# The mixers' triangular inverse on smaller tiles of the array, its substitution on GpSimd, and the last chain's rank

## The chip, the cores and the metric

The kernel runs on one core of one Trainium2 chip. The core has TensorE (matrix products), VectorE and ScalarE (element-wise work), GpSimd, SyncE (which here only issues DMAs) and 16 DMA engines. The metric is the device time of one execution in microseconds; where several executions are shown it is their median.

## The reference

Two transformer-like blocks run one after the other on one sequence of 256 tokens with 2048 features, all in float32. The first has a gated linear recurrence, an attention with forget gates and a pooling branch, then a feed-forward network. The second normalises, projects once, and runs two mixers on the projection: an RWKV-7 recurrence over 16 heads of 64 and a gated delta rule over 8 heads of 128; then an output product and a feed-forward network. The change touches only the mixers. What they compute is this:

```python
def rwkv7_recurrence(r, w, k, v, a, b):
    def step(S, inp):
        r_t, w_t, k_t, v_t, a_t, b_t = inp
        Sa = jnp.einsum('bhvk,bhk->bhv', S, a_t)
        S = S * w_t[:, :, None, :] + Sa[..., None] * b_t[:, :, None, :] + v_t[..., None] * k_t[:, :, None, :]
        return S, jnp.einsum('bhvk,bhk->bhv', S, r_t)
...
def gated_delta_rule_chunked(q, k, v, g, beta):
    ...
    L = jnp.where(strict, jnp.einsum('bhnid,bhnjd->bhnij', k_beta, k) * gamma, 0.0)
    rhs = jnp.concatenate([v_beta, k_beta * jnp.exp(g)[..., None]], axis=-1)
    sol = lax.linalg.triangular_solve(L + eye, rhs, left_side=True, lower=True, unit_diagonal=True)
...
y_a, v_first = rwkv7_mixer(p_rwkv, ...)
y_b = gdn_mixer(p_gdn, ...)
y = jnp.concatenate([y_a, y_b], axis=-1).astype(x.dtype)
x = x + y @ w_out[l]
```

The kernel computes both recurrences in two chunks of 128 tokens. In each chunk and head the dependence of a token on the earlier ones is a triangular matrix of 128 x 128 with ones on its diagonal, which has to be inverted: 32 of them for RWKV, 16 for the delta rule.

## The kernel before

Nearly all the time is products with streamed weights. A weight tile of 128 x 1024 float32 (512 KB) comes from DRAM as `raw` (L310). ScalarE rounds it to `hi` (L314), VectorE takes the rest as `lo` (`sub`, L206), and TensorE multiplies a 512-column product with `hi` and a 256-column one with `lo` (`product`, `mm`, L233) for each 128 x 128 block. The activations `h` are split in the same way. These products write tiles called `ps`; below they are the main stream. About 0.35 us of TensorE go by for one pair of them.

The mixers (`mixers`) run between about 1600 and 2117 us. Four rounds `g` each have an RWKV group (two heads in each of two fronts, so eight matrices, `ab`) and a gated-delta group (one front, four matrices, `gab`). A front makes its projections with the main stream and then a small graph that ends in the matrices; RWKV's come from the products `pf<-ar,bt` and `pf<-ar,kt`. After a group's front, `diagonals` starts on its 16 x 16 diagonal blocks: eight DMAs bring them to DRAM (`scr`, L1105), one brings them back with one block on each partition (`d`, L1107), 15 steps of a back substitution of a product and an addition each invert all blocks at once (`etmp`, `e`, on VectorE), and two DMAs bring the result through DRAM (`scs`, L1122) to `cmp` (L1124), a column of blocks for each matrix.

While the next group's front runs, `step` works off the group before: `merged_inverse` for four matrices at a time (two calls for an RWKV group, one for a gated-delta group, so three in a round and twelve in all), and behind it the rest of the chain (`rwkv_back`, `gdn_back`), which writes the mixer's output. An inverse call takes the 16-row blocks to 32, 64 and 128 rows. Each of the first two levels masks the matrix, multiplies twice (four products of 128 x 128 each time, on `pb` tiles) and transposes; the last one works with 64 x 64 quarters. A float32 product is two passes on TensorE.

The order of instructions on each engine is set when the program is built, by a scheduler that takes the code's order and a rank: `back_ahead = 205`, `diag_ahead = 129` and the like put what stands in a `high_priority` block so many places ahead. So the products of the chains stand in between products of the main stream, and where one of them has to wait, the main stream behind it on TensorE waits too. SyncE issues the weight loads and the DMAs of `diagonals` in one queue. The last group's chain runs beside `out2_first`, the first part of the output product.

Of the kernel before, what the change touches and what calls it, by code (L numbers as in the profile page):

```python
# [7 lines left out]
F32 = mybir.dt.float32  # L8
# [7 lines left out]
P = 128  # L16
# [135 lines left out]
def constants():  # L152
    i = np.arange(P)
    r, c = i[:, None], i[None, :]
    sel1 = np.zeros((P, 8), np.float32)
    sel2 = np.zeros((P, 8), np.float32)
    for h in range(8):
        sel1[h, h] = 1.0
        sel2[32 + h, h] = 1.0
    c1 = ((i >= 32) & (i < 40)).astype(np.float32)[:, None]  # L160
    c2 = (i < 8).astype(np.float32)[:, None]
    up = (c > r).astype(np.float32)
    upi = (c >= r).astype(np.float32)
    same = lambda b: (r // b == c // b)
    lev = lambda b: (same(2 * b) & ~same(b) & (c > r)).astype(np.float32)
    return [
        ("ident", np.eye(P)), ("ones", np.ones((P, P))),
        ("causal", np.where(c <= r, 0.0, -1e30)), ("causalT", np.where(r <= c, 0.0, -1e30)),
        ("head64", same(64).astype(np.float32)),
        ("nsel1", -sel1), ("sel2", sel2), ("c1", c1), ("c2", c2),  # L170
        ("atmask", np.concatenate([up, upi], 1)),
        ("lev16", lev(16)), ("lev32", lev(32)), ("lev64", lev(64)), ("blk16", same(16).astype(np.float32)),
        ("id16", np.broadcast_to(np.eye(16).reshape(1, 256), (P, 256))),
    ]


def ffn_out(w):
# [5 lines left out]
class Prog:  # L183
# [95 lines left out]
    def setup(self):  # L279
        nc, a = self.nc, self.a  # L280
        self.const = self.pool("const", 1)
        self.rawp, self.hip, self.lop = (self.pool(n, b) for n, b in zip(("raw", "hi", "lo"), self.rings))
        self.evp = self.pool("ev", 3)
        self.bigp = self.pool("big", 1)
        self.psum = self.pool("psum", 8 - sum(self.pbufs), PSUM)
        self.psx = self.pool("psx", 1, PSUM)
        self.dram = self.pool("dram", 1, DRAM)
        self.par = self.const.tile([P, a["par"].shape[1]], F32, name="par")
        self.cst = self.const.tile([P, a["cst"].shape[1]], F32, name="cst")
# [505 lines left out]
class Block2(Block1):  # L795
# [102 lines left out]
    def mixers(self, rh, st):  # L898
# [3 lines left out]
        self.gp = self.pool("mxg", 1, st=st)  # L902
        self.parted = True
        self.narrow = self.nar3
        ps = self.product([(w2[0], KT)], rh)
        self.norm2_end()
        self.omu = kp.tile([P, 27], F32, name="omu")
# [25 lines left out]
            self.step(pend, first=True)  # L933
        self.narrow = self.nar4
        self.out2_first()
        self.step(pend)

    def step(self, pend, first=False):
# [14 lines left out]
                        self.gdn_back(g, fr, xx)  # L953

    back_ahead = 205
    diag_ahead = 129
    front_ahead = 0

    def shifted(self, ps, o, j):

        t = self.w(S + 1, "shf")
        self.G.memset(t[:, 0:1], 0.0)
        self.scaled(ps, t[:, 1:])
        self.act(o, t[:, 1:], AF.Copy, scale=self.omu[:, j:j + 1])
        self.stt(o, t[:, :S], self.p("mu_rkv", j), o, ALU.mult, ALU.add)
# [39 lines left out]
    def rwkv_rest(self, j, slot, t, slots):  # L1005
# [5 lines left out]
        self.G.memset(cw[:, :, 0:1], 0.0)  # L1011
# [86 lines left out]
    def diagonals(self, slots, gdn):  # L1098
# [15 lines left out]
        self.V.tensor_copy(x, self.c("id16")[:8 * n].rearrange("p (i j) -> p i j", i=16))  # L1114
# [12 lines left out]
    def merged_inverse(self, slots, half, gdn):  # L1127

        full, cm, p0 = slots["ab"], slots["cm"], 4 * half
        q4 = lambda z: z.rearrange("p (q t) -> p q t", q=4)  # L1130
        xt = self.gp.tile([P, 4, P], F32, name="xt", tag="xt", bufs=2)
        x = self.gp.tile([P, 4, P], F32, name="xn", tag="xn", bufs=2)
        self.mul(xt.rearrange("p q (b j) -> p q b j", b=8),
                 cm[:, p0:p0 + 4].rearrange("p q (a j) -> p q a j", a=1).to_broadcast([P, 4, 8, 16]),
                 self.c("blk16").rearrange("p (a b j) -> p a b j", a=1, b=8).to_broadcast([P, 4, 8, 16]))
        px = self.psx_tile(True)
        for q in range(4):
            self.tr(px[:, q * P:(q + 1) * P], xt[:, q])
        self.A.copy(x, q4(px))
        beta = lambda q, rows=slice(0, P): self.nbt[rows, q % 2, 2 * gdn + q // 2:2 * gdn + q // 2 + 1]  # L1140
        for lev in ("lev16", "lev32"):
            off = self.tp.tile([P, 4, P], F32, name="off", tag="w4")
            self.mul(off, full[:, p0:p0 + 4], self.bc(lev, 4))
            pm = self.psx_tile(True)
            for q in range(4):
                self.mm(pm[:, q * P:(q + 1) * P], off[:, q], x[:, q])
            m1 = self.tp.tile([P, 4, P], F32, name="m1", tag="w4")
            pt = self.psx_tile(True)
            if gdn is None:
                self.add(m1, q4(pm), self.bc("ident", 4))  # L1150
            else:
                for q in range(4):
                    self.act(m1[:, q], pm[:, q * P:(q + 1) * P], AF.Copy, scale=beta(q))
            for q in range(4):
                self.mm(pt[:, q * P:(q + 1) * P], m1[:, q], xt[:, q])
            if gdn is None:
                self.A.copy(xt, q4(pt))
            else:
                self.add(xt, q4(pt), xt)
            px = self.psx_tile(True)  # L1160
            n = P if lev == "lev16" else 64
            for q in range(4):
                self.T.transpose(px[:n, q * n:(q + 1) * n], xt[:n, q, :n], self.c("ident")[:n, :n])
            self.A.copy(x[:n, :, :n], q4(px[:n, :4 * n]))

        lo, hi = slice(0, 64), slice(64, P)
        pm = self.psx_tile(True)
        for q in range(4):
            self.mm(pm[hi, q * 64:(q + 1) * 64], full[lo, p0 + q, hi], x[lo, q, lo])
        m1 = self.tp.tile([P, 4, P], F32, name="m1", tag="w4")  # L1170
        if gdn is None:
            self.A.copy(m1[hi, :, :64], q4(pm[hi, :S]))
        else:
            for q in range(4):
                self.act(m1[hi, q, :64], pm[hi, q * 64:(q + 1) * 64], AF.Copy, scale=beta(q, hi))
        for q in range(4):
            self.mm(pm[lo, S + q * 64:S + (q + 1) * 64], m1[hi, q, :64], xt[hi, q, hi])
        self.A.copy(xt[lo, :, hi], q4(pm[lo, S:]))
        return xt

# [89 lines left out]
    def gdn_front(self, i, rh, w2, slots):  # L1270
        gp = self.gp

        big = gp.tile([P, 6, S], F32, name="gbig", tag="gbig")
        for b in range(6):
            ps = self.product([(w2[27 + 6 * i + b], KT)], rh)
            if b >= 4:
                self.scaled(ps, big[:, b])
                continue
            t = self.w(S + 3, f"gc{b}")
            self.G.memset(t[:, :3], 0.0)  # L1280
# [155 lines left out]
```

## Time and profile before

| | |
|---|---|
| median of 3 runs | 2921.1 us (2919.22 to 2923.79) |
| the profiled execution's own time | 2924.65 us |
| its span | 2922.9 us |
| its mean granted clock | 0.998 of full speed |
| TensorE, VectorE, ScalarE, GpSimd busy | 99%, 68%, 52%, 1% |
| mean DMA rate | 176 GB/s |

The span is cut into stretches by time: the two that matter for the change are the mixers' from 1606 to 2117 us and, inside it, the first inverse at 1686 us. Rows of an engine in order of time have the start, the duration, the engine, the line of the kernel, the operation, the names written and read, and, in brackets, how long the engine was idle before it and what ended that. Successive products overlap on TensorE, so the time that one takes from the engine is read from start to start and not from its duration.

### The profile page before, as it was taken

The numbers are of one execution on the slowest core, as the hardware profiler recorded it, in microseconds if no ns is written. First come the engines' busy times: TensorE is split into PE (matmuls) and PEld (weight loads), VectorE is DVE, ScalarE is ACT, GpSimd is POOL, SyncE is SP. The second block draws the span as 40 slices with busy tenths as digits, with TensorE's granted clock in tenths as the row PEclk, the third lists the DMA queues.
The fourth block names the chain that finished last, engine by engine and source line by source line (L and its number), as shares of the span: only waits on it lengthen the run. The fifth ranks groups of instructions, "written<-read, shape, count | busy, mean of one in ns | idle before, by whom it ended". The sixth has DMA issues, their size and how long they took to land. (4 is left out here: it accounts for less than half of the span.)

```text
span 2922.9 us, 46401 instructions
## 1 busy us (share of the span) xinstructions
PE 2888.2 (99%) x17676; PEld 2540.8 (87%) x17676; DVE 1990.9 (68%) x3393; ACT 1506.3 (52%) x2448; POOL 21.5 (1%) x88
## 2 busy tenths in 40 slices
PE   8999999999999999999999999999999999999998
PEld 8999988888888888888888878887888888888887
DVE  7855766666766665666667878888776665566665
ACT  6644454444554444444556555666564444444454
POOL 0000000000000000000000000000010000000000
PEclk9999999999999999999999999999999999999999
DMA  6544555555655556555565423233465555655554
GB/s 232 183 160 154 173 188 191 190 188 189 231 190 189 189 177 192 201 191 191 180 206 186 148 87 122 92 130 110 145 207 189 190 186 182 201 191 190 184 177 159
DMA packets 178047, 515.78 MB, mean 176 GB/s; under 512 B 32024, under 2 KB 59040, under 8 KB 177568
## 3 DMA queue, kind: packets, MB, share of 16 engines
q1 hardware_dynamic: 177536, 511.80, 51.9%
q8 instruction: 138, 2.26, 0.3%
q10 hardware_dynamic: 288, 1.02, 0.1%
q14 instruction: 85, 0.70, 0.1%
HBM read 505.66 MB, written 7.09 MB: 175 GB/s over the span
## 5 line engine op out<-in xcount | busy, mean ns | idle before, releaser
L233 PE MATMUL ps<-h,hi 128*128 128x512 f32 (+1 forms) x5904 | 1801.0, 366 | 1.2 <-DVE xp L206 0.9
L206 DVE TENSOR_TENSOR lo<-raw,hi 128x1024 fp32r<-128x1024 f32 (+2 forms) x1028 | 1156.6, 1125 | 759.0 <-ACT hi L314 754.9
L314 ACT CAST hi<-raw 128x1024 fp32r<-128x1024 f32 (+2 forms) x1028 | 997.2, 971 | 1193.3 <-issue 663.8
L233 PE MATMUL ps<-h,lo 128*128 128x256 f32 x5152 | 1410.6, 282 | 0.9 <-DVE lo L206 0.6
L233 PEld LDWEIGHTS ps<-h,hi 128*128 128x128 f32 x5904 | 1041.6, 188 | 164.4 <-issue 6.0
L233 PEld LDWEIGHTS ps<-h,lo 128*128 128x128 f32 x5152 | 969.5, 188 | 29.4 <-issue 2.4
L233 PE MATMUL ps<-mid,hi 128*128 128x512 f32 (+1 forms) x1452 | 486.2, 385 | 0.0
L233 PE MATMUL ps<-mid,lo 128*128 128x256 f32 x1408 | 386.1, 281 | 0.0
L233 PEld LDWEIGHTS ps<-mid,hi 128*128 128x128 f32 x1452 | 265.4, 188 | 50.5
L233 PEld LDWEIGHTS ps<-mid,lo 128*128 128x128 f32 x1408 | 265.1, 188 | 5.3
L206 DVE TENSOR_TENSOR t<-ps,s 128x256 f32<-128x256 f32 x323 | 134.8, 417 | 0.0
L381 ACT COPY s<-ps 128x256 f32<-128x256 f32 x323 | 118.3, 367 | 0.0
L233 PE MATMUL ps<-merged,hi 128*128 128x512 f32 x256 | 88.0, 392 | 0.0
L233 PE MATMUL ps<-merged,lo 128*128 128x256 f32 x256 | 69.0, 280 | 0.0
L233 PEld LDWEIGHTS ps<-merged,hi 128*128 128x128 f32 x256 | 47.0, 188 | 9.6 <-DVE merged L206 0.2
L233 PE MATMUL ps<-y,hi 128*128 128x512 f32 (+1 forms) x160 | 49.3, 359 | 1.7 <-ACT hi L314 1.4
L233 PEld LDWEIGHTS ps<-merged,lo 128*128 128x128 f32 x256 | 48.1, 188 | 1.3
L233 PE MATMUL ps<-yg,hi 128*128 128x512 f32 (+1 forms) x160 | 48.6, 354 | 0.0
L233 PE MATMUL ps<-yb,hi 128*128 128x512 f32 x128 | 46.1, 393 | 0.0
L233 PE MATMUL ps<-yc,hi 128*128 128x512 f32 x128 | 46.1, 393 | 0.0
L233 PE MATMUL ps<-ya,hi 128*128 128x512 f32 x128 | 45.9, 391 | 0.0
L206 DVE TENSOR_TENSOR t<-ps,xres 128x256 f32<-128x256 f32 x78 | 33.1, 424 | 12.9 <-PE ps L233 7.0
(383 smaller groups left out, 2307.8 us busy)
## 6 DMA issues: line engine op xcount, KB each, us to landing
raw<-wg SPq DMA_DIRECT2D x352, 512.0 KB, 4.2
raw<-w SPq DMA_DIRECT2D x292, 512.0 KB, 3.6
raw<-wd SPq DMA_DIRECT2D x128, 512.0 KB, 3.5
raw<-wbr SPq DMA_DIRECT2D x48, 512.0 KB, 3.5
raw<-wo SPq DMA_DIRECT2D x48, 512.0 KB, 4.3
raw<-wd SPq DMA_DIRECT2D x128, 192.0 KB, 3.1
raw<-wo SPq DMA_DIRECT2D x32, 256.0 KB, 3.2
xin<-x SPq DMA_DIRECT2D x4, 512.0 KB, 6.4
```

What stands on the lines that cost most here:

```text
L206: return (e or self.V).tensor_tensor(out=o, in0=x, in1=y, op=op)
L233: return self.T.matmul(o, lhsT=l, rhs=r, start=start, stop=stop, skip_group_check=True)
L314: self.A.copy(hi, raw)
L381: self.A.copy(s[:rows], ps[:rows, S:])
```

## The change

Three things change, and some small ones with them.

1. `merged_inverse` no longer works on 128 x 128 matrices. The blocks of a level stand as [128, 4, 32] or [128, 4, 64], one block below the other. Products of 32 x 32 or 64 x 64 use only the rows and columns of TensorE at that block (`tiles`). The first transpose is VectorE's, in blocks of 32; the others fall away, since each level computes both the blocks and their transposes (`merge`). The masks of 128 columns go, and smaller constants come.
2. In `diagonals` the substitution runs on GpSimd. It also copies the blocks above the diagonal that the two levels multiply into tiles `off` that are zeroed once. Three small memsets go from GpSimd to VectorE (L962, L1011 and L1280 of before).
3. The last chain gets the rank 2000 where the others have 205.

The constants' tile has 320 columns less of content and 320 of padding, so it is as large as before.

```diff
...
-        ("lev16", lev(16)), ("lev32", lev(32)), ("lev64", lev(64)), ("blk16", same(16).astype(np.float32)),
+        ("id64", np.tile(np.eye(64), (2, 1))), ("id32", np.tile(np.eye(32), (4, 1))),
+        ("blk16", diag_blocks(same(16).astype(np.float32), 32)), ("blk32", diag_blocks(same(32).astype(np.float32), 64)),
...
+        self.offs = {}
+        for n in (8, 4):
+            for w in (32, 64):
+                off = self.offs[n, w] = kp.tile([P, n, w], F32, name=f"off{n}_{w}")
+                self.G.memset(off, 0.0)
...
         self.out2_first()
+        self.back_ahead = self.last_ahead
         self.step(pend)
...
     back_ahead = 205
+    last_ahead = 2000
     diag_ahead = 129
...
-        self.G.memset(t[:, 0:1], 0.0)
+        self.V.memset(t[:, 0:1], 0.0)
...
-            self.stt(d, d, -1.0, nb.to_broadcast([8 * n, 16, 16]), ALU.mult, ALU.mult)
+            self.ts(nb, nb, -1.0, e=self.G)
+            self.mul(d, d, nb.to_broadcast([8 * n, 16, 16]), self.G)
...
-            self.mul(o, d[:, :t, t:t + 1].to_broadcast([8 * n, t, w]), x[:, t:t + 1, t:].to_broadcast([8 * n, t, w]))
-            self.add(x[:, :t, t:], x[:, :t, t:], o)
+            self.mul(o, d[:, :t, t:t + 1].to_broadcast([8 * n, t, w]), x[:, t:t + 1, t:].to_broadcast([8 * n, t, w]), self.G)
+            self.add(x[:, :t, t:], x[:, :t, t:], o, self.G)
...
+        for w in (32, 64):
+            off = slots[w] = self.offs[n, w]
+            for r in range(0, P, w):
+                up, right = slice(r, r + w // 2), slice(r + w // 2, r + w)
+                self.G.tensor_copy(off[up, :, w // 2:], full[up, :, right])
...
+        def tiles(out, left, right, w, rows=P):
+            for q in range(4):
+                for r in range(0, rows, w):
+                    r = slice(r, r + w)
+                    self.mm(out[r, q], left[r, q], right[r, q])
+
+        def merge(x, w, rows):
+
+            off = slots[w][:, p0:p0 + 4]
             pm = self.psx_tile(True)
...
+            tiles(q4(pm[:, :4 * w]), off, x[:, 1], w)
+            m = self.tp.tile([P, 4, 64], F32, name="m1", tag="m4", bufs=3)[:, :, :w]
             if gdn is None:
...
+                self.add(m, q4(pm[:, :4 * w]), one(self.c(f"id{w}"), w))
             else:
                 for q in range(4):
...
+                    self.stt(m[:, q], pm[:, q * w:(q + 1) * w], beta(q), self.c(f"id{w}"), ALU.mult, ALU.add)
+            pt = self.psx_tile(True)
+            pt = pt[:, :8 * w].rearrange("p (a q t) -> p a q t", a=2, q=4)
+            tiles(pt[:, 0], m, x[:, 0], w)
+            tiles(pt[:, 1], x[:, 0], m, w, rows)
+            return pt
+
+        xt = self.gp.tile([P, 4, P], F32, name="xt", tag="xt", bufs=2)
+        self.V.memset(xt[hi, :, lo], 0.0)
+        x = self.gp.tile([P, 2, 4, 32], F32, name="xa", tag="xa", bufs=2)
...
+        self.V.transpose(x[:, 1].rearrange("p q t -> p (q t)"), x[:, 0].rearrange("p q t -> p (q t)"))
+        pt = merge(x, 32, P)
+        x = self.gp.tile([P, 2, 4, 64], F32, name="xb", tag="xb", bufs=1)
+        for j in range(2):
+            self.mul(x[:, j].rearrange("p q (b t) -> p q b t", b=2),
+                     pt[:, j].rearrange("p q (b t) -> p q b t", b=1).to_broadcast([P, 4, 2, 32]),
+                     self.c("blk32").rearrange("p (a b t) -> p a b t", a=1, b=2).to_broadcast([P, 4, 2, 32]))
+        pt = merge(x, 64, 64)
+        for r in (lo, hi):
+            self.A.copy(xt[r, :, r], pt[r, 0])
+        y = self.tp.tile([P, 4, 64], F32, name="xc", tag="m4", bufs=3)
+        self.V.tensor_copy(y[lo], pt[lo, 1])
...
```

TensorE, first inverse call of the second round, before: `pb` rows are the inverse's, `ps` rows the main stream's; the rows left out between them are main-stream products.

```order
L236 MATMUL pb<-cst,xt 128x128 x4
...
L233 MATMUL pb<-xn,off 128x128 x4
...
L233 MATMUL pb<-xt,m_18602 128x128 x4
...
L1163 MATMUL pb<-cst,xt 128x128 x4
...
L233 MATMUL pb<-xn,off 128x128 x4
...
L233 MATMUL pb<-xt,m_18623 128x128 x4
...
L1163 MATMUL pb<-cst,xt 64x64 x4
...
L233 MATMUL pb<-xn,ab 64x64 x4
...
L233 MATMUL pb<-xt,m_18642 64x64 x4
```

Nine groups, the two quarter products at the end among them. In this round 174 main-stream products stand between the last `ar,kt` product and the first row of this fence; in the other rounds it is 141, 174 and 168.

The same call on TensorE, after:

```order
L238 MATMUL pb<-xa,off_32_15951 32x32 x16
...
L238 MATMUL pb<-xa,m_18746 32x32 x16
L238 MATMUL pb<-m_18746,xa 32x32 x16
...
L238 MATMUL pb<-xb,off_64_15953 64x64 x8
...
L238 MATMUL pb<-xb,m_18793 64x64 x8
L238 MATMUL pb<-m_18793,xb 64x64 x4
...
L238 MATMUL pb<-xc,ab 64x64 x4
...
L238 MATMUL pb<-xt,m_18817 64x64 x4
```

Three transposes and four groups of 128 x 128 products have gone, and four groups of small products have come. The first row now stands 115 main-stream products behind the last `ar,kt` one (in the four rounds 125, 115, 119 and 109). In the second gated-delta group 67 products stand between the last `kq` product and the first one of the inverse, where 99 stood.

SyncE's queue in the second round, before: `raw<-w` are weight loads, the others the DMAs of `diagonals`.

```order
L1105 DMA scr_18147<-ab 16x8x16 x8
L310 DMA raw<-w 128x1024 x2
L1107 DMA d<-scr_18147 64x256
L310 DMA raw<-w 128x1024 x6
L1122 DMA scs_18191<-e 64x256
L310 DMA raw<-w 128x1024
L1124 DMA cmp<-scs_18191 128x8x16
```

The load of the blocks stands behind two weight loads, and the write of the inverted blocks behind six more.

The same place on SyncE, after:

```order
L1118 DMA scr_18279<-ab 16x8x16 x8
L316 DMA raw<-w 128x1024
L1120 DMA d<-scr_18279 64x256
L316 DMA raw<-w 128x1024 x3
L1136 DMA scs_18323<-e 64x256
L316 DMA raw<-w 128x1024
L1138 DMA cmp<-scs_18323 128x8x16
```

One weight load fewer stands ahead of the load of the blocks, and three instead of six ahead of the write. Whatever the write waits for, the weight loads behind it wait for too.

GpSimd in the mixers, after (before, there are only memsets here): a gated-delta group's copies and the start of its substitution.

```order
L1128 COPY e<-cst 32x256
L1145 COPY off_32_15955<-gab 16x4x16 x4
L1145 COPY off_64_15957<-gab 32x4x32 x2
L211 TENSOR_TENSOR d<-d,nbd 32x256
L211 TENSOR_TENSOR etmp<-d,e 32x15
L211 TENSOR_TENSOR e<-e,etmp 32x15
L211 TENSOR_TENSOR etmp<-d,e 32x14x2
L211 TENSOR_TENSOR e<-e,etmp 32x14x2
```

The copies stand before the first operation that needs the blocks back. GpSimd's rows of a group stand together; among those of a gated-delta group there is one small operation on the next group's `nbd`.

## Rows read from the trace of the kernel before

**Rows 1.** The page: busy time by engine, and one costly group.

```profile
PE 2888.2 (99%) x17676; PEld 2540.8 (87%) x17676; DVE 1990.9 (68%) x3393; ACT 1506.3 (52%) x2448; POOL 21.5 (1%) x88
...
L206 DVE TENSOR_TENSOR t<-ps,s 128x256 f32<-128x256 f32 x323 | 134.8, 417 | 0.0
```

**Rows 2.** Stretches: length, busy PE, PEld, DVE, ACT, POOL, clock, DMA share, GB/s.

```profile
1606.00:2117.00 511.00, 502.56 (x3161) 414.80 (x3160) 405.20 (x1015) 301.17 (x605) 4.85 (x44) 1.00 0.37 119
1683.00:1686.20 3.20, 0.43 (x3) 0.10 (x1) 0.68 (x2) 1.36 (x3) 0.00 (x0) 0.96 0.63 233
1686.20:1690.00 3.80, 3.73 (x18) 3.44 (x19) 2.75 (x6) 1.18 (x3) 0.10 (x1) 0.59 0.07 25
```

**Rows 3.** TensorE in order of time at the first inverse.

```profile
1686.27 1.11 PE L236 MATMUL pb<-cst,xt 128*128 128x128 f32 x4 [2.84 <-DVE xt L206]
```

**Rows 4.** TensorE in order of time, 1717 to 1724 us.

```profile
1717.22 0.39 PE L233 MATMUL ps<-h,hi 128*128 128x512 f32 x1
1717.45 1.07 PE L233 MATMUL pb<-xn,off 128*128 128x128 f32 x8
...
1718.48 0.40 PE L233 MATMUL ps<-h,hi 128*128 128x512 f32 x1
...
1721.12 0.39 PE L233 MATMUL ps<-h,hi 128*128 128x512 f32 x1
1721.44 0.41 PE L1163 MATMUL pb<-cst,xt 64*64 64x64 f32 x4
...
1722.01 0.40 PE L233 MATMUL ps<-h,hi 128*128 128x512 f32 x1
...
1722.36 0.39 PE L233 MATMUL ps<-h,hi 128*128 128x512 f32 x1
1722.68 0.68 PE L233 MATMUL pb<-xn,ab 64*64 64x64 f32 x8
...
1723.51 0.39 PE L233 MATMUL ps<-h,hi 128*128 128x512 f32 x1
```

**Rows 5.** TensorE in order of time at 2011 us.

```profile
2011.34 0.48 PE L233 MATMUL pf<-ar,bt 64*128 64x256 f32 x1
2011.34 0.48 PE L233 MATMUL pf<-ar,kt 64*128 64x256 f32 x1
2011.66 0.38 PE L233 MATMUL pf<-ar,bt 64*128 64x256 f32 x1
```

**Rows 6.** Instructions on tile etmp: ns shortest/median/longest, first and last start, forms.

```profile
L206 DVE TENSOR_TENSOR etmp<-d,e x120: 152/198/220, 1666.3 to 2089.0; 64x15 f32<-64x15 f32 x8, 64x28 f32<-64x28 f32 x8, 64x39 f32<-64x39 f32 x8, 64x48 f32<-64x48 f32 x8
```

**Rows 7.** TensorE in order of time, second round.

```profile
1771.20 0.80 PE L233 MATMUL pf<-ar,kt 64*128 64x256 f32 x3
...
1804.57 0.66 PE L236 MATMUL pb<-cst,xt 128*128 128x128 f32 x4
```

**Rows 8.** VectorE in order of time, second round.

```profile
1784.14 0.18 DVE L206 TENSOR_TENSOR etmp<-d,e 64x15 f32<-64x15 f32 x1 [0.62 <-DMA d<-scr]
```

**Rows 9.** SyncE's queue in order of time, second round.

```profile
1773.18 3.66 SPq L1105 DMA_DIRECT2D scr<-ab  x8
1776.94 2.85 SPq L310 DMA_DIRECT2D raw<-w  x2
1780.06 0.47 SPq L1107 DMA_DIRECT2D d<-scr  x1
1782.11 15.01 SPq L310 DMA_DIRECT2D raw<-w  x6
1798.40 0.46 SPq L1122 DMA_DIRECT2D scs<-e  x1
```

**Rows 10.** GpSimd's groups: count | busy us, mean ns | idle us before, releasers.

```profile
L206 POOL TENSOR_TENSOR acc<-acc,q 128x256 f32<-128x256 f32 x15 | 13.8, 920 | 154.7 <-ACT q L230 154.7
L962 POOL MEMSET shf<- 128x1 f32 x27 | 2.8, 110 | 1550.9 <-PE pf L233 1096.2 <-PE ps L233 424.3 <-DVE rs_w L206 14.2
```

**Rows 11.** TensorE's groups by shape: the first transposes.

```profile
L236 PE MATMUL pb<-cst,xt 128*128 128x128 f32 x48 | 8.4, 292 | 3.5 <-DVE xt L206 3.5
```

More of the change, by code (lines that the diff above doesn't have):

```diff
@@ L164, in constants @@
     same = lambda b: (r // b == c // b)
-    lev = lambda b: (same(2 * b) & ~same(b) & (c > r)).astype(np.float32)
     return [
@@ L171, in constants, with diag_blocks @@
         ("atmask", np.concatenate([up, upi], 1)),
-        ("lev16", lev(16)), ("lev32", lev(32)), ("lev64", lev(64)), ("blk16", same(16).astype(np.float32)),
+        ("id64", np.tile(np.eye(64), (2, 1))), ("id32", np.tile(np.eye(32), (4, 1))),
+        ("blk16", diag_blocks(same(16).astype(np.float32), 32)), ("blk32", diag_blocks(same(32).astype(np.float32), 64)),
         ("id16", np.broadcast_to(np.eye(16).reshape(1, 256), (P, 256))),
     ]
+def diag_blocks(m, n):
+    return np.concatenate([m[i:i + n, i:i + n] for i in range(0, P, n)], 0)
 def ffn_out(w):
@@ L288, in setup @@
         self.par = self.const.tile([P, a["par"].shape[1]], F32, name="par")
-        self.cst = self.const.tile([P, a["cst"].shape[1]], F32, name="cst")
+        self.cst = self.const.tile([P, a["cst"].shape[1] + 320], F32, name="cst")[:, :a["cst"].shape[1]]
         nc.scalar.dma_start(out=self.par, in_=a["par"])
@@ L1010, in rwkv_rest @@
         cw, e1, e2 = (ch(self.w(2 * (P + 1), n)) for n in ("cw", "e1", "e2"))
-        self.G.memset(cw[:, :, 0:1], 0.0)
+        self.V.memset(cw[:, :, 0:1], 0.0)
         for c in range(2):
@@ L1125, in diagonals @@
         slots["cm"] = cm
+        for w in (32, 64):
[3 more added lines that the diff above has]
+                self.G.tensor_copy(off[up, :, w // 2:], full[up, :, right])
     def merged_inverse(self, slots, half, gdn):
         full, cm, p0 = slots["ab"], slots["cm"], 4 * half
+        lo, hi = slice(0, 64), slice(64, P)
         q4 = lambda z: z.rearrange("p (q t) -> p q t", q=4)
-        xt = self.gp.tile([P, 4, P], F32, name="xt", tag="xt", bufs=2)
@@ L1132, in merged_inverse @@
[L1132 to L1139, printed above, removed]
-        beta = lambda q, rows=slice(0, P): self.nbt[rows, q % 2, 2 * gdn + q // 2:2 * gdn + q // 2 + 1]
@@ L1141, in merged_inverse @@
-        for lev in ("lev16", "lev32"):
-            off = self.tp.tile([P, 4, P], F32, name="off", tag="w4")
-            self.mul(off, full[:, p0:p0 + 4], self.bc(lev, 4))
+        one = lambda z, w: z.rearrange("p (a t) -> p a t", a=1).to_broadcast([P, 4, w])
+        beta = lambda q, rows=slice(0, P): self.nbt[rows, q % 2, 2 * gdn + q // 2:2 * gdn + q // 2 + 1]
+        def tiles(out, left, right, w, rows=P):
[3 more added lines that the diff above has]
+                    self.mm(out[r, q], left[r, q], right[r, q])
@@ L1144, in merged_inverse @@
+        def merge(x, w, rows):
+            off = slots[w][:, p0:p0 + 4]
             pm = self.psx_tile(True)
[L1145 to L1148, printed above, removed]
+            tiles(q4(pm[:, :4 * w]), off, x[:, 1], w)
+            m = self.tp.tile([P, 4, 64], F32, name="m1", tag="m4", bufs=3)[:, :, :w]
             if gdn is None:
-                self.add(m1, q4(pm), self.bc("ident", 4))
+                self.add(m, q4(pm[:, :4 * w]), one(self.c(f"id{w}"), w))
@@ L1151, in merged_inverse @@
             else:
                 for q in range(4):
[L1153 to L1163, printed above, removed]
@@ new lines, in merged_inverse @@
+        self.V.memset(xt[hi, :, lo], 0.0)
+        x = self.gp.tile([P, 2, 4, 32], F32, name="xa", tag="xa", bufs=2)
+        self.mul(x[:, 0].rearrange("p q (b j) -> p q b j", b=2),
+                 cm[:, p0:p0 + 4].rearrange("p q (a j) -> p q a j", a=1).to_broadcast([P, 4, 2, 16]),
+                 self.c("blk16").rearrange("p (a b j) -> p a b j", a=1, b=2).to_broadcast([P, 4, 2, 16]))
+        self.V.transpose(x[:, 1].rearrange("p q t -> p (q t)"), x[:, 0].rearrange("p q t -> p (q t)"))
+        pt = merge(x, 32, P)
@@ L1167, in merged_inverse @@
+        self.V.tensor_copy(y[lo], pt[lo, 1])
         pm = self.psx_tile(True)
         for q in range(4):
-            self.mm(pm[hi, q * 64:(q + 1) * 64], full[lo, p0 + q, hi], x[lo, q, lo])
-        m1 = self.tp.tile([P, 4, P], F32, name="m1", tag="w4")
+            self.mm(pm[hi, q * 64:(q + 1) * 64], full[lo, p0 + q, hi], y[lo, q])
+        m1 = self.tp.tile([P, 4, 64], F32, name="m1", tag="m4", bufs=3)
         if gdn is None:
-            self.A.copy(m1[hi, :, :64], q4(pm[hi, :S]))
+            self.A.copy(m1[hi], q4(pm[hi, :S]))
@@ L1173, in merged_inverse @@
         else:
             for q in range(4):
[L1175 removed]
+                self.act(m1[hi, q], pm[hi, q * 64:(q + 1) * 64], AF.Copy, scale=beta(q, hi))
         for q in range(4):
[L1177 removed]
+            self.mm(pm[lo, S + q * 64:S + (q + 1) * 64], m1[hi, q], xt[hi, q, hi])
         self.A.copy(xt[lo, :, hi], q4(pm[lo, S:]))
@@ L1279, in gdn_front @@
             t = self.w(S + 3, f"gc{b}")
-            self.G.memset(t[:, :3], 0.0)
+            self.V.memset(t[:, :3], 0.0)
             self.scaled(ps, t[:, 3:])
```

4 lines of the change are left out of this document (1 added, 3 removed).

## The prediction

> **What bounds the kernel now.** I read the page first, then busy times by stretch, then the order of time on TensorE, VectorE and SyncE inside the mixers, since every edit lies there. TensorE is busy for 99% of the span, VectorE for 68% [rows 1]. The stretch from 1606 to 2117 us holds the eight mixer groups and the first part of the output product. In it TensorE is busy 502.56 of 511 us, so 8.4 us is all the idle time that relief elsewhere can give back; VectorE is at 405 us there, ScalarE at 301, GpSimd at 4.85 [rows 2]. So the change pays by what it takes off TensorE's own row of work, and costs by every wait that it puts into it. One wait is there already: at the first inverse TensorE stands 2.84 us until the diagonal blocks are back [rows 3]. In the 3.8 us behind it the granted clock is 0.59, so mostly the lower of its two levels (1.2 and 2.4 GHz), which costs 0.41 x 3.8 = 1.6 us more [rows 2].
>
> **The change part by part.**
>
> *The products of the inverse.* It is called twelve times (three calls in each of four rounds). A call is nine groups on TensorE now, and seven are replaced: three of transposes and four of four 128x128 products (eight passes, two to each fp32 product). The last two, 64x64, stay. I price a group from the start of the 512-wide product ahead of it to the start of the one behind it, less 0.35 us for the two products that fall in between anyway; this takes in the drain and the weights that could not be loaded ahead. Four products: 1718.48 - 1717.22 - 0.35 = 0.91 us. The 64-row transposes: 1722.01 - 1721.12 - 0.35 = 0.54. A 64x64 group of eight passes: 1723.51 - 1722.36 - 0.35 = 0.80 [rows 4]. I take the 128-row transposes at 0.54 too. Removed per call: 4 x 0.91 + 3 x 0.54 = 5.26 us.
>
> Added per call are four groups: 16 products 32x32, then 32 of them, then eight 64x64, then twelve. A 128-column pass takes 0.91 / 8 = 0.114, so a 64-column one half of that, 0.058 rounded up, and 0.80 - 8 x 0.058 = 0.34 us is the fixed price of a small-tile group. Passes on different row tiles run side by side: the `ar,bt` and `ar,kt` products stand on two halves of the rows and start in the same hundredth of a microsecond, 0.48 long each, the next pair 0.32 later [rows 5]. No row has a 32-row tile. By halving again, a pass takes 0.032; the bounds are 0.008 (four side by side) and 0.058 (nothing gained from the shorter row), and I take 0.012, between two and four side by side. That gives 0.34 + 32 x 0.012 = 0.72 and 0.34 + 64 x 0.012 = 1.11, and for the 64-row groups (two side by side, but the last eight passes on one tile) 0.34 + 16 x 0.029 = 0.80 and 0.34 + 16 x 0.029 + 8 x 0.058 = 1.27. Sum 3.90 us, saved 1.36 per call, 16.3 in twelve. The new order cuts groups into pieces at twelve more places (0.34 each, 4.1); the old one cut a few cheaper ones, so I charge 3.5. **TensorE: -12.8 us.**
>
> *The substitution on GpSimd.* In each of eight groups 30 dependent small operations leave VectorE, 0.198 us each [rows 6]. VectorE's 47 us are worth nothing by themselves, since TensorE's work hides them. What counts is when the blocks come back. In the second round the chain of now is: the last product that feeds it, from 1771.20 to 1772.00 [rows 7], eight DMAs out, one back, the first operation at 1784.14 [rows 8], the DMA behind the last at 1798.40 [rows 9], one more DMA, the transposes at 1804.57 [rows 7]. Without the substitution that is 12.1 + 6.2 = 18.3 us. The new order has one weight load less ahead of the DMA back, on which SyncE stood until 1780.06 [rows 9], so I take 17.0. GpSimd's two-input operation on 256 elements takes 0.920 us, its memset of one column 0.110 [rows 10]. The new ones have 15 to 64 elements, 45 on average: by a straight line 0.25 us. I take 0.24, or 7.2 us for thirty; the bounds are 3.3 (all like the memset) and 27.6 (all like the large one).
>
> So the blocks are needed 17.0 + 7.2 = 24.2 us after the last product that feeds them. In the new order TensorE arrives sooner: between the last `ar,kt` and the first product of the inverse stand 125, 115, 119 and 109 products of the main stream in the four rounds, where 141, 174, 174 and 168 stood. At 0.35 us a pair, and 1.5 us of other work, that is 23.3, 21.6, 22.3 and 20.5 us: waits of 0.9, 2.6, 1.9 and 3.7, in sum 9.1, less 3.0 for the first one's of now: +6.1. The gated-delta groups have more work in between; only the second is tight (67 products where 99 stood), and I put its wait at 2.3, from 0 to 4. Behind TensorE's waiting product stands the main stream, behind VectorE's the split of the next weights, behind SyncE's waiting DMA the weight loads; a ring of four loads is held ahead, each worth 2.8 us of products, so a few microseconds there are covered. **Waits: +8.4 us.** One wait of about 3 us is there before and after, so the clock's 1.6 us stay.
>
> A rule that speaks against this edit: the Trainium skill (GPSIMD Engine Reference, 4.1 Engine selection) puts element-wise work on VectorE, as GpSimd is about twice as slow with two inputs. The trace agrees: 0.920 us against VectorE's 0.417 at 128x256 [rows 1, 10]. By that rule thirty operations would take 11.8 us and the whole change some 25 us more than now.
>
> *The rest.* 51 memsets of 0.1 us go from GpSimd to VectorE, hidden as above. VectorE and ScalarE lose masks, adds and copies over 128x512 for pieces a quarter or half as large; six copies per group go to GpSimd and stand before the substitution, while its data travel. All this is bounded by TensorE's idle time outside the counted wait, 8.4 - 3.0 = 5.4 us; I credit half. **Relief: -2.5 us**, from 0 to -5.4. The last chain, ranked first, ends earlier, but the second part of the output product starts only when the first has ended, so that earns nothing: the chain's cover is that first part. If its blocks are late it costs a wait like the others, at most the 3.7 above.
>
> **Sum:** -12.8 + 8.4 - 2.5 = -6.9 us. The profiled execution took 2924.65 us (span 2922.9, 1.75 around it), which gives 2917.8; the median of the three runs shown lies 3.5 us lower, at 2921.1, and gives 2914.
>
> **Rivals.**
>
> *GpSimd too slow (slower).* If it stands to VectorE as at 256 elements, 0.920 / 0.417 = 2.2 times 0.198, an operation takes 0.44 us and the substitution 13.1. The rounds wait 17.0 + 13.1 less TensorE's way: 6.8, 8.5, 7.8 and 9.6, in sum 32.7, less 3.0; the second gated-delta group waits 8.2, the last about 4. That is +41.9, and four more waits long enough for the clock to fall as it does now, +6.4. With -12.8 and -2.5 it gives +33: 2954. It decides from where the five waits eat the 6.9 us, 1.4 each: 8.6 us for thirty, 0.29 an operation. For it: the steps depend on each other, and a busy VectorE reads the same memory. Against: VectorE itself needed 14.3 us for 5.9 us of operations, since they stood between others, and GpSimd has nothing else to do.
>
> *Small tiles don't run side by side (slower).* At 0.032 a 32-row pass and 0.058 a 64-row one the groups take 1.36, 2.39, 1.27 and 1.73: 6.75 per call, 1.49 more than what goes. Twelve calls +17.9, cuts +3.5, waits +8.4, relief -2.5: +27, 2948. At 0.058 for all it is 2978. For it: the rows show two tiles side by side and never four, and these two write different tiles of the accumulator. Against: nothing in the new groups depends on another tile.
>
> The Trainium skill (TensorEngine Tiling (Array Packing), Gotcha 1: PSUM Pressure) says that different row tiles cannot access one PSUM bank at the same time. The new groups write one bank from four row tiles, on different partitions; no row here shows that case. By that rule this rival would come true.
>
> *All fits (faster still).* Four side by side (-17.5 with the cuts), no wait left at the blocks (-3.0 and the clock's -1.6), the idle time given back (-5.4): -27, 2894. For it: the order of now is well timed, since in all twelve calls TensorE idled 3.5 us at the first transposes, 2.84 of it in the first [rows 3, 11], and the new one may be so again.
>
> **How the numbers follow.** The forecast has 0.42, with a range of its own from 2904 to 2923; GpSimd too slow 0.27; no overlap 0.13; all fits 0.18. A change under 0.2% (5.8 us) can't be told from none. Of the forecast's share about 0.25 lies beyond that, 0.17 within; of the slow GpSimd's 0.04 lies within. So faster 0.43, same 0.21, slower 0.36. The range reaches from the good case to near the bad ones: 2893 to 2950.
>
> **What would show it.** Right: 32x32 groups of 0.7 to 1.1 us, GpSimd's operations at about 0.24 us from start to start, waits of 1 to 4 us at the inverse's first product, VectorE's busy time some 50 us lower. Wrong: steps of 0.3 us or more with waits over 5 us and a lower clock behind them, or 32x32 groups over 1.4 us.

## The result: slower by 1.9%, and where the time went

The changed kernel takes 2975.8 us (median of 5 runs, 2972.6 to 2979.4) against 2921.1 before: 1.0187 times as long, interval 1.0176 to 1.0198. The forecast was 2914, its range 2893 to 2950. What came true is the first rival, "GpSimd too slow", which had a chance of 0.27 and a time of 2954, and it came at a higher price than it was given.

First the page and the waits of the kernel after (engine, tile and line, what it waited for; us in total, times, longest), beside [rows 1, 11]:

```profile
PE 2886.3 (97%) x18780; PEld 2528.7 (85%) x18780; DVE 1954.2 (66%) x3252; ACT 1482.3 (50%) x2389; POOL 143.2 (5%) x345
```

```profile
DVE xa L211 <- DMA cmp<-scs: 58.3, 8, 10.5
PE pb L238 <- DVE xa L1186: 51.6, 6, 10.8
PE pb L238 <- DVE z L211: 5.5, 2, 3.3
```

TensorE idles 51.6 us at the first product of an inverse where it idled 3.5 before, in six places, and 5.5 at two later products of the chain (`pb<-z,xt`), where no wait stood before. It is busy about as long as before, although it has less to do. The busy times by stretch show why (columns as in [rows 2]; the mixers are longer now, and the second and third rows are 4 us around the end of two of the waits, 0.6 to 0.7 us of the wait and the work behind it):

```profile
1606.00:2166.00 560.00, 500.84 (x4257) 401.78 (x4255) 364.24 (x862) 274.54 (x545) 122.49 (x302) 0.94 0.35 106
...
1809.30:1813.30 4.00, 3.27 (x73) 2.60 (x77) 2.11 (x6) 0.00 (x0) 0.00 (x0) 0.50 0.48 174
...
2079.30:2083.30 4.00, 3.40 (x98) 2.95 (x102) 2.08 (x8) 1.87 (x2) 0.00 (x0) 0.50 0.42 99
```

At each of the six waits such a stretch of 4 us has a granted clock of 0.50 to 0.57, so it is near its lower level. The same place on TensorE in the second round, which [rows 7] shows for before:

```profile
1799.94 0.39 PE L238 MATMUL ps<-h,hi 128*128 128x512 f32 x1
1810.03 0.66 PE L238 MATMUL pb<-xa,off 32*32 32x32 f32 x32 [9.70 <-DVE xa L1186]
1810.62 0.58 PE L238 MATMUL ps<-h,lo 128*128 128x256 f32 x1
1811.00 0.63 PE L238 MATMUL ps<-h,hi 128*128 128x512 f32 x1
```

The main stream's products behind the wait take 0.63 us where they took 0.39. What TensorE waits for is on GpSimd, VectorE and SyncE (answering [rows 6, 8, 9]; GpSimd's operations first, then VectorE's splits of the weights at the same time, then SyncE's queue):

```profile
L211 POOL TENSOR_TENSOR etmp<-d,e x120: 204/290/1574, 1663.8 to 2133.8; 64x15 f32<-64x15 f32 x8, 64x28 f32<-64x28 f32 x8, 64x39 f32<-64x39 f32 x8, 64x48 f32<-64x48 f32 x8
```

```profile
1789.11 1.20 POOL L211 TENSOR_TENSOR etmp<-d,e 64x15 f32<-64x15 f32 x1 [7.18 <-DMA d<-scr]
1790.39 0.34 POOL L211 TENSOR_TENSOR e<-e,etmp 64x15 f32<-64x15 f32 x1
...
1791.86 0.25 POOL L211 TENSOR_TENSOR etmp<-d,e 64x39 f32<-64x39 f32 x1
1792.18 1.13 POOL L211 TENSOR_TENSOR e<-e,etmp 64x39 f32<-64x39 f32 x1
...
1796.40 0.30 POOL L211 TENSOR_TENSOR e<-e,etmp 64x60 f32<-64x60 f32 x1
1796.78 0.30 POOL L211 TENSOR_TENSOR etmp<-d,e 64x63 f32<-64x63 f32 x1
...
1803.81 0.21 POOL L211 TENSOR_TENSOR e<-e,etmp 64x15 f32<-64x15 f32 x1
```

```profile
1789.00 1.23 DVE L211 TENSOR_TENSOR lo<-raw,hi 128x1024 fp32r<-128x1024 f32 x1 [0.65 <-ACT hi L320]
...
1791.89 1.29 DVE L211 TENSOR_TENSOR lo<-raw,hi 128x1024 fp32r<-128x1024 f32 x1 [0.23 <-ACT hi L320]
```

```profile
1779.21 4.75 SPq L1118 DMA_DIRECT2D scr<-ab  x8
...
1804.05 0.46 SPq L1136 DMA_DIRECT2D scs<-e  x1
```

The thirty operations run from 1789.11 to 1804.02: 14.9 us; the eight groups take 12.7 to 15.2. Two things make that up. Undisturbed, one of the larger operations follows another after 0.38 us (1796.40 to 1796.78: 0.30 of work and 0.08 between), and after 0.29 us for the smallest. And one that meets VectorE's weight split ends only just behind it: the 1.20 at 1789.11 and the 1.13 at 1792.18 lie on the two splits. Of the 240 operations 24 last over 1 us, and all 24 overlap a split. From the end of the last product that feeds the blocks to the first product of the inverse it is now 31.6 us in this round, and TensorE is there after 21.9.

In this round the chain is no slower than it was: before, the same way took 32.6 us (1772.00 to 1804.57, [rows 7]), and the substitution on VectorE 14.2 of them, against 14.9 now. What is new is that TensorE comes for the blocks some 10 us earlier.

To see all terms, I added TensorE's time from start to start between the same two main-stream products in each trace, before and behind the mixers, by what the product belongs to (us). Idle is where the next product starts over 0.7 us later, less the product's own time; a wait counted in this way is 0.15 to 0.2 us longer than the idle time in a row, and the waits in the expectations and in the text on the experiments are counted so. The `gab` products of the inverse, 2.4 us in each kernel, stand under other mixer products.

| kernel | sum | main stream | inverse | other mixer products | idle |
|---|---|---|---|---|---|
| before | 601.2 | 401.0 | 68.4 | 122.2 | 9.5 |
| after | 652.2 | 406.9 | 49.7 | 132.9 | 62.7 |
| sub_vector | 583.2 | 402.5 | 47.2 | 123.1 | 10.4 |
| all_vector | 581.0 | 403.8 | 47.5 | 120.8 | 8.8 |
| gp_later | 637.3 | 413.1 | 49.4 | 124.3 | 50.6 |
| last205 | 678.6 | 428.8 | 59.4 | 130.6 | 59.8 |
| sub_vector_l205 | 601.9 | 413.6 | 54.0 | 122.8 | 11.4 |

After against before: the inverse saves 18.7, the idle time costs 53.2, and the same other work takes 16.6 us longer, much of it at the lower clock: together +51.0. Not all of the lower clock is behind a wait: from 1882 to 1886 us it is 0.50 with TensorE busy for 4.00 of 4.00 us, where 64-row products of a front stand one by one among a chain's 128-row ones.

### The profile page after: what moved, and what is told of

Same layout as the page of the kernel before. It is cut to its first block, busy times and chain, and to the rows that moved or that the text cites. A ratio compares the mean times of both kernels' runs of the same rounds, so it can differ in the third digit from the quotient of the medians.

```text
span 2971.9 us, 48569 instructions
## 1 busy us (share of the span) xinstructions
PE 2886.3 (97%) x18780; PEld 2528.7 (85%) x18780; DVE 1954.2 (66%) x3252; ACT 1482.3 (50%) x2389; POOL 143.2 (5%) x345
## 4 chain that ended last, share of the span: by engine, by line
PE 87%; POOL 3%; DMA 3%; DVE 2%; ACT 2%; issue 1%; SPq 0%; ACTq 0%; POOLq 0%; DVEq 0%
PE ps L238 81%; PE pb L238 3%; PE pf L238 2%; POOL e L211 2%; POOL etmp L211 2%; DMA cmp<-scs 1%; DMA d<-scr 1%; DVE lo L211 1%; ACT hi L320 1%; DMA scs<-e 0%; SPq L1118 0%; PE pf L241 0%; DMA up<-up 0%; DMA raw<-wo 0%; ACT h L235 0%
## 5 line engine op out<-in xcount | busy, mean ns | idle before, releaser
L238 PE MATMUL pb<-xa,off 32*32 32x32 f32 x384 | 6.8, 218 | 51.6 <-DVE xa L1186 51.6
L238 PE MATMUL ps<-yg,hi 128*128 128x512 f32 (+1 forms) x160 | 50.6, 366 | 0.0
L211 POOL TENSOR_TENSOR e<-e,etmp 64x15 f32<-64x15 f32 (+7 forms) x120 | 49.2, 410 | 9.2
```

Source lines behind the costliest of these rows:

```text
L211: return (e or self.V).tensor_tensor(out=o, in0=x, in1=y, op=op)
L238: return self.T.matmul(o, lhsT=l, rhs=r, start=start, stop=stop, skip_group_check=True)
```

## The experiments

Theory A: the inverse on small tiles saves what it seems to; the loss is the wait for GpSimd's substitution, at an order that lets TensorE arrive before it ends. B: the small tiles or their cuts lose it. C: the last chain's rank loses it. D: GpSimd's work slows VectorE and with it the main stream.

**sub_vector**, the substitution back on VectorE (with the start of `e` and the scaling by beta), all else as changed:

```diff
-            self.mul(o, d[:, :t, t:t + 1]..., x[:, t:t + 1, t:]..., self.G)
-            self.add(x[:, :t, t:], x[:, :t, t:], o, self.G)
+            self.mul(o, d[:, :t, t:t + 1]..., x[:, t:t + 1, t:]...)
+            self.add(x[:, :t, t:], x[:, :t, t:], o)
```

> The kernel after, with the substitution (30 operations a group, the start of e and the scaling by beta) back on VectorE; the compact inverse, the copies on GpSimd and the last chain's rank stay. The scheduler then puts 158, 151, 181 and 146 main-stream products between a round's last feeding product and the first product of its inverse, where the kernel after has 119, 115, 119, 109. Theory A (the whole loss is the wait for GpSimd's substitution, 14 to 15 us a group, at an order that leaves TensorE only 21 to 23 us): waits at the first products fall from 52.6 us in sum to under 12, the inverse's groups keep their 19 us less than before: 2905 to 2922 us. Theory B (the small tiles, their cuts or the smaller pieces on VectorE lose the time): still over 2945 us. Theory C (the last chain's rank loses it): over 2955 us.

2905.96 us, 0.9944 of before (0.9931 to 0.9956): 70 us less than the kernel after, by moving 30 small operations a group and with them the order. Its first products (group by shape; count, busy, mean ns, idle before):

```profile
L238 PE MATMUL pb<-xa,off 32*32 32x32 f32 x384 | 5.4, 193 | 4.4 <-DVE xa L1185 4.4
```

VectorE's thirty operations do not end sooner than GpSimd's: 12.2 to 14.9 us in the RWKV groups, 17.7 to 18.7 in the others, as they stand between other work. What differs is that the order gives them that time: 158, 151, 181 and 146 products instead of 119, 115, 119 and 109 (this count starts a few products later in the first round than the 125 given with the change). A holds, B and C fall. VectorE's split of 128 x 1024 takes 1.22 us on average in these mixers and 1.23 in those of the kernel after, so D has next to nothing to work with.

**old_inv_gp**, the other half alone: the old inverse, only the substitution on GpSimd (the same lines of before with `self.G`).

> The kernel before with the substitution alone moved to GpSimd; the inverse stays on 128 x 128 products. TensorE then arrives 110, 115, 119 and 118 main-stream products after the feed instead of 141, 174, 174, 168. Theory A: first-transpose waits of 8 to 11 us in each round and some more in the gated-delta groups, 2965 to 2990 us. Theory B (the loss is the compact inverse's): within 15 us of 2921. Theory C (the last chain): within 15 us of 2921.

2993.15 us, 1.0245 (1.0231 to 1.0259). A holds, a little over its range; five more stops of 1.9 to 7.2 us stand at the gated-delta groups, so B and C fall here too. Its first transposes, to hold against [rows 11]:

```profile
L236 PE MATMUL pb<-cst,xt 128*128 128x128 f32 x48 | 9.8, 328 | 42.0 <-DVE xt L206 42.0
```

**gp_later**, GpSimd kept, the inverse's first products tied behind later main-stream ones:

```diff
+            if w == 32 and half == 0:
+                with self.tc.issue_after(self.mains[min(slots["from"], len(self.mains) - 1)]):
+                    tiles(q4(pm[:, :4 * w]), off, x[:, 1], w)
...
+            if g < 3:
+                self.early = [self.product([(w2[9 + 6 * g + b], KT)], rh) for b in range(2)]
```

> The kernel after with GpSimd's substitution kept, but the inverse's first products are tied behind later main-stream products, and two of the next RWKV front's projections are issued ahead of the inverse in rounds 1 to 3: 125, 186, 176 and 120 products where 119, 115, 119 and 109 stood, and 113, 115, 115, 161 in the gated-delta groups where 88, 67, 88, 101 stood. Theory A (GpSimd's latency costs only where TensorE arrives before it ends): the waits of 9.87 and 8.29 in rounds 2 and 3 and the 5.29 of the second gated-delta group fall under 1 us, rounds 1 and 4 keep theirs of 8 to 10: 2940 to 2956 us. Theory D (GpSimd's work slows VectorE and so the main stream, wherever the inverse stands): the time stays within 8 us of 2976.

2960.96 us: 15 less than after, not the 20 to 36 expected of A and not within D's 8. The products of rounds 2 and 3 no longer wait for the blocks, but they came to stand somewhere else. VectorE and then TensorE of gp_later in the second round:

```profile
1803.96 0.50 DVE L211 TENSOR_TENSOR xa<-cmp,cst 128x128 f32<-128x128 f32 x2 [9.67 <-DMA cmp<-scs]
```

```profile
1805.84 0.58 PE L238 MATMUL ps<-h,lo 128*128 128x256 f32 x1 [6.22 <-DVE lo L211]
```

In VectorE's order the next weight split stands behind the multiplication `xa`, which waits for `cmp`, and the main stream runs dry. The wait was moved, not hidden.

**gp_later_all**, with that multiplication tied behind later splits too, and the two DMAs behind the substitution issued by GpSimd:

```diff
+        with self.tc.issue_after(lo_at):
+            self.mul(x[:, 0]..., cm[:, p0:p0 + 4]..., self.c("blk16")...)
...
-        self.nc.sync.dma_start(out=cm, in_=scr2.rearrange("p b i j -> (b i) p j"))
+        self.nc.gpsimd.dma_start(out=cm, in_=scr2.rearrange("p b i j -> (b i) p j"))
```

> As gp_later, but the first multiplication of the inverse on VectorE is tied behind later weight splits too, and the two DMAs behind the substitution are issued by GpSimd instead of SyncE, so that neither VectorE's splits nor the weight loads stand behind a wait for GpSimd. Theory A (in gp_later the wait only moved to the in-order queues of VectorE and SyncE: xa waited 9.67 us for cmp and the main stream ran out of splits): the 6.4 and 6.3 us stops of rounds 2 and 3 and the 3 to 4 us ones in the gated-delta groups fall under 1.5 us each, rounds 1 and 4 keep 8 to 9: 2932 to 2950 us, against 2961 of gp_later. Rival E (DMAs of GpSimd are slower or fight its work): cmp lands later, 2955 us or more.

2961.26 us, no better. The first products of rounds 2 and 3 now wait for 2.0 and 1.7 us, but three of the gated-delta groups stop for 5.6 to 5.8 where gp_later had 2.8 to 4.4. VectorE and TensorE there:

```profile
1859.86 0.29 DVE L211 TENSOR_TENSOR xa<-cmp,cst 128x128 f32<-128x128 f32 x1 [6.57 <-DMA cmp<-scs]
```

```profile
1860.47 0.80 PE L238 MATMUL pb<-s,ar 128*128 128x128 f32 x2 [5.64 <-DVE s L223]
```

Now a chain's own `s` stands behind `xa`. The time lies in rival E's range, and a part of E is there: in rounds 2 and 3 `xa` starts 6.0 us after the last operation of the substitution, where it was 5.1 and 5.2 in gp_later, and the substitution takes 16.9 and 16.7 us, where it took 14.0 and 15.0. So this run does not tell A from E. That an order exists which hides GpSimd's 14 us was not shown.

**last205**, the kernel after with the last chain's rank back at 205 (`last_ahead = 205`):

> The kernel after with the last chain's rank back at 205: 142 instead of 101 products ahead of the last inverse, the rest as it is. Theory A: the last wait of 9.68 us falls to 0 to 3, and what follows it is unchanged: 2964 to 2971 us. Theory C (the rank itself costs more than the wait): under 2960. If the chain's earlier end is worth what the wait costs: 2972 to 2980.

2997.37 us, 21.6 more than after: all three expectations missed. The last wait only shrank (9.7 to 7.9 us) and moved from the inverse's product to one of the main stream, which waits for VectorE's split behind `xa`. And the order now mixes the last inverse's products one by one with the main stream. By stretch and in order of time:

```profile
2150.20:2154.70 4.50, 4.50 (x27) 2.68 (x26) 2.44 (x4) 0.93 (x1) 0.00 (x0) 1.00 0.69 200
...
2160.00:2190.00 30.00, 30.00 (x126) 17.63 (x127) 7.46 (x17) 3.03 (x4) 0.00 (x0) 0.52 0.18 49
2190.00:2200.00 10.00, 10.00 (x71) 7.20 (x70) 4.30 (x10) 3.68 (x9) 0.00 (x0) 1.00 0.39 113
```

```profile
2150.21 0.24 PE L238 MATMUL pb<-xa,off 32*32 32x32 f32 x2
2150.39 0.39 PE L238 MATMUL ps<-y,lo 128*128 128x256 f32 x1
...
2154.57 0.24 PE L238 MATMUL pb<-xa,off 32*32 32x32 f32 x2
...
2156.16 0.31 PE L238 MATMUL pb<-xa,off 32*32 32x32 f32 x2
2156.41 0.58 PE L238 MATMUL ps<-y,lo 128*128 128x256 f32 x1
2156.92 0.31 PE L238 MATMUL pb<-xa,off 32*32 32x32 f32 x2
2157.16 0.80 PE L238 MATMUL ps<-yg,hi 128*128 128x512 f32 x1
```

This costs twice. At the full clock eight single products of the inverse (two passes each) and four pairs of the main stream take 4.36 us (2150.21 to 2154.57); less 0.35 a pair that is 0.37 us for a single product, and 32 passes in one run take 0.38 us together (shown further below). 43 products stand alone here, so by this estimate some 16 us go by without the clock. Then the clock falls, with TensorE busy all the while: from 2160 to 2190 it is busy for 30 of 30 us at a clock of 0.52, and the clock is at 1.00 again behind the last single product. Theory F: the rank is worth something only because it keeps the small products together. G: it is worth it anywhere. Two runs:

**before_last2000**, before with the rank alone (`self.back_ahead = 2000` ahead of the last `step`):

> The kernel before with the last chain's rank at 2000 and nothing else: 115 instead of 144 products ahead of its last inverse, whose first transposes stand together (before, they stood one by one between main-stream products). Theory F (the rank is worth 21 us in the kernel after only since it keeps 32 x 32 products from being mixed one by one with the main stream, which runs at 0.50 of the clock there): here within 5 us of the kernel before, 2916 to 2926, or a few us longer if the blocks come late. Rival G (the rank itself ends the chain earlier, worth its 21 us anywhere): 2895 to 2905.

2923.19 us, 1.0001 (0.9992 to 1.0010): as F expects, and far from G's 2895 to 2905.

**sub_vector_l205**, sub_vector with `last_ahead = 205`:

> sub_vector with the last chain's rank back at 205: the order has its 32 x 32 products in one run of 15 and one alone, not one by one. Theory F: within 6 us of sub_vector, 2900 to 2912. Rival G (the rank itself): 2920 to 2930.

2922.24 us, 16.3 more than sub_vector. The number given for F was wrong, and the time lies in the range given for G. The run of 15 products and one alone is only the first group of the order; in the two groups behind it nearly all products stand one by one:

```profile
2086.00:2110.00 24.00, 24.00 (x93) 13.54 (x94) 5.02 (x9) 2.71 (x3) 0.00 (x0) 0.50 0.22 65
```

```profile
2090.15 0.31 PE L238 MATMUL pb<-xa,m 32*32 32x32 f32 x2
2090.39 0.58 PE L238 MATMUL ps<-y,lo 128*128 128x256 f32 x1
2090.90 0.31 PE L238 MATMUL pb<-xa,m 32*32 32x32 f32 x2
2091.14 0.80 PE L238 MATMUL ps<-y,hi 128*128 128x512 f32 x1
```

The time does not decide between F and G, but the table does: of the 18.7 us more than in sub_vector 17.9 lie on the inverse and the main stream and 1.0 on idle time, and a chain that only ended later would leave TensorE idle. So F's mechanism is there twice, and G is out. 27 products stand alone here, 10 us at 0.37. The clock's part is less certain: in last205 it falls some 4.5 us into the alternation, with no idle time in between; here it falls as the alternation begins, behind a wait of 1.6 us, but sub_vector has a wait of 2.0 us at the same place and keeps 1.00. What in the alternation lowers the clock was not separated.

**split_halves**, the kernel after with VectorE's split in two:

```diff
-                self.sub(lo, raw, hi.bitcast(F32))
...
+                    for s in range(0, n, n // 2):
+                        s = slice(s, s + n // 2)
+                        self.sub(lo[:, s], raw[:, s], hi[:, s].bitcast(F32))
```

> The kernel after with VectorE's weight split in the mixers as two operations of 128 x 512 instead of one of 128 x 1024. The order moves too (TensorE's inverses stand closer to the feed), so only GpSimd's operations are read. Theory H (an operation of GpSimd that meets a split stands until that VectorE operation ends, then runs): the long ones of 1.05 to 1.57 us become 0.5 to 0.85, and a group's 30 operations take 12 to 14 us instead of 12.7 to 15.2. Rival I (both share the memory, each at its part): the long ones keep over 1 us.

H: operations on a split now last 0.5 to 0.83 us, all but four. Those four, each the first of an RWKV group, begin under another VectorE operation and stand through both halves, for 1.0 to 1.6 us; H does not explain them. The groups take 11.9 to 13.9 us. GpSimd, and VectorE at the same time:

```profile
1799.79 0.60 POOL L211 TENSOR_TENSOR e<-e,etmp 64x39 f32<-64x39 f32 x1
1800.46 0.59 POOL L211 TENSOR_TENSOR etmp<-d,e 64x48 f32<-64x48 f32 x1
1801.14 0.28 POOL L211 TENSOR_TENSOR e<-e,etmp 64x48 f32<-64x48 f32 x1
```

```profile
1799.55 1.38 DVE L211 TENSOR_TENSOR lo<-raw,hi 128x512 fp32r<-128x512 f32 x2 [0.29 <-ACT hi L320]
```

The first operation ends 0.60 us after its start, well before the second of the two splits does: GpSimd got in between them. The Trainium skill (SBUF — State Buffer, Who interferes with whom) says that a VectorE instruction with two inputs in SBUF contends with a GpSimd instruction that reads SBUF, over a port pair that is an exclusive lock; these rows agree. The one run took 2970.1 us; the order was another, so the time says nothing of the split.

**all_vector**, sub_vector with the copies of the off-diagonal blocks on VectorE too:

```diff
-                self.G.tensor_copy(off[up, :, w // 2:], full[up, :, right])
+                self.V.tensor_copy(off[up, :, w // 2:], full[up, :, right])
```

> sub_vector with the copies of the blocks above the diagonal moved from GpSimd to VectorE too, so that GpSimd has nothing left of the inverse. Theory A (only the serial latency of the substitution costs; the copies run while the blocks travel): within 4 us of sub_vector, 2902 to 2910. Rival D (any work of GpSimd in the mixers slows VectorE's splits): under 2900.

2902.3 us, 0.9930 (0.9917 to 0.9942), the fastest of all, 20 us under before: as A expected, D's gain isn't there.

**sub_vector_b150** and **sub_vector_b300**, sub_vector with `back_ahead` 150 and 300:

> sub_vector with the rank of all chains but the last at 150 instead of 205: 158, 165, 182, 160 products ahead of the first product of each round's inverse where 158, 151, 181, 146 stood, and no more pieces of the inverse among the main stream (87 in both). The waits of 1.57, 0.90 and 2.19 us at those products become 1.5, 0 and 0: 2901 to 2906 us, if nothing else moves; the rank before is worth what it was (2906) if the chain's later end costs as much.

> sub_vector with that rank at 300: 158, 165, 180, 167 products, 87 pieces. Same reasoning, 2901 to 2906 us.

2904.25 us (0.9935, 0.9922 to 0.9947) and 2907.01 (0.9942, 0.9929 to 0.9956): the waits moved (1.6, 1.7, 0 and 0 us; 1.3, 2.1, 1.7 and 0 us, where 1.5, 0 and 0 were expected), and neither time can be told from sub_vector's.

## Why the prediction was wrong, step by step

- **"I take 0.24, or 7.2 us for thirty."** This step failed, and it turned the sign. Start to start it is 0.29 to 0.39 us undisturbed, and with two to four of over 1 us in each group the thirty took 12.7 to 15.2 us. The bounds (3.3 to 27.6) held it; the value taken from a straight line between two rows left out the gap of 0.08 between dependent operations and the splits of VectorE. The rival's 13.1 was close.
- **"17.0 + 7.2 = 24.2 us after the last product."** The 17.0 was right: 31.6 less 14.9 is 16.7. So was TensorE's way, 23.3, 21.6, 22.3 and 20.5 forecast and 23.2, 21.9, 23.2 and 20.8 measured. So the failed term is the 7.2 alone: TensorE's earlier arrival was set against a chain that was to be 8 us shorter than before and got 1 us shorter.
- **Its price, 2954.** Short by 22 us, of which the table shows 18. The inverse has -18.7 where this rival had -16.3. Idle time has +53.2 where it had 41.9 - 2.5 = 39.4: the six waits sum to 51.6, not 41.9 + 3.0, two more stand at `pb<-z,xt` (5.5), and no relief came. The other work has +16.6 where 3.5 for cuts and 6.4 for the clock were counted. The range should have reached past this rival, which sat outside it at 0.27.
- **"TensorE: -12.8 us."** Right in sign, too small in size. The inverse saves 18.7, and 21.2 where no wait disturbs it (sub_vector), where 16.3 were forecast; the main stream, where the cuts show, is 1.5 longer there, not 3.5. In the kernel after, at the full clock, and in the last row the kernel before, behind the product at 1722.68 of [rows 4]:

```profile
1819.05 0.68 PE L238 MATMUL pb<-xc,ab 64*64 64x64 f32 x8
1819.65 0.51 PE L238 MATMUL ps<-h,hi 128*128 128x512 f32 x1
...
1830.03 0.45 PE L238 MATMUL pb<-xa,off 32*32 32x32 f32 x32
1830.41 0.70 PE L238 MATMUL pf<-kq 128*128 128x256 f32 x2
```

```profile
1723.28 0.38 PE L233 MATMUL ps<-h,lo 128*128 128x256 f32 x1
```

  The price of a 64 x 64 group was right: the group that stays takes 0.60 us from start to start in both kernels, and its 0.80 has what the products on either side lose in it. Too high was a 32-row pass: 32 of them take 0.38 us from start to start, and four passes start within 31 ns, so 0.008 us a pass, the prediction's lower bound, and not 0.012. With 96 such passes in a call that is an estimated 4.6 us in twelve calls.
- **"Small tiles don't run side by side"**: refuted; 0.38 / 32 = 0.012 us a pass with everything, where this rival had 0.032 and the fixed price besides, and within a group four passes start 7 ns apart. The rule of the Trainium skill (TensorEngine Tiling (Array Packing), Gotcha 1: PSUM Pressure) that row tiles cannot access one bank at a time does not bind here: these four write one bank, on different partitions.
- **"Relief: -2.5 us."** None: where the long waits are gone the idle time is 10.4 (sub_vector), against 9.5 before.
- **"The last chain, ranked first, ... earns nothing."** Wrong in the compact kernel: it is worth 21.6 us with GpSimd's substitution and 16.3 with VectorE's, since it keeps the small products together; right in the kernel before (1.0001).

Compact products without the rank (sub_vector_l205) and the rank without them (before_last2000) both give nothing against before; together they give 16 us, and GpSimd's substitution takes 70 away.

## What to carry to other kernels

Price a chain of small dependent operations on another engine by its start-to-start time, gap and collisions included, and compare it with the time at which the engine that needs the result arrives in the new order, not with the time the chain took before. The order can move with the engine: here the same chain on GpSimd brought its consumer forward on the bottleneck, from 146 to 181 products behind the feed to 109 to 119, as if it had become shorter, so the bottleneck paid the wait (what the scheduler counts for an operation of GpSimd is not shown here). Tying the consumer alone behind later work moved the wait to the next engine's queue. And read the order of small products for whether they stand together or one by one among the large ones: here that decided 16 to 22 us.

## What the runs showed of the hardware that was not expected

- 32 x 32 float32 passes on the four diagonal tiles of the array start 7 ns apart, 31 ns for four and 0.38 us for 32 of them, at the full clock.
- A single 32 x 32 product between 128 x 128 ones takes 0.37 us of TensorE's time at the full clock (last205).
- Such an alternation ran at a clock of 0.50 to 0.52 for 24 to 30 us with TensorE busy throughout. In sub_vector, where all but a few of the 32 x 32 products stand in pieces of four and more, the clock over the mixers is 1.00:

```profile
1606.00:2104.00 498.00, 489.91 (x4294) 395.45 (x4294) 399.39 (x1124) 278.11 (x547) 18.68 (x48) 1.00 0.41 124
```

- A GpSimd operation that meets VectorE's split of 128 x 1024 takes 1.1 to 1.6 us instead of 0.2 to 0.3.
